# A half step by seven products: block columns first, a pinned order of products, norm parts from unshifted tokens

## The chip, the cores and the metric

One core of a Trainium2 chip runs the whole program in one launch. The metric is the device time of that launch in microseconds. TensorE multiplies; VectorE (DVE), ScalarE (ACT) and GpSimd (POOL) work on SBUF and, the first two, on PSUM; SyncE (SP) issues most DMAs, POOL some.

## The reference

Two layers over 256 context and 256 latent tokens of width 1024. Each layer is a SwiGLU half step, a token mixing (mLSTM and latent attention), and another half step; each part gets its tokens through a norm with shift and scale. What the change touches is one half step:

```python
def _rmsnorm(x, g):
    y = xf * lax.rsqrt(jnp.mean(xf * xf, axis=-1, keepdims=True) + EPS)
    return (y * g.astype(jnp.float32)).astype(x.dtype)

def _modulate(h, shift, scale):
    return h * (1 + scale) + shift

def _swiglu(h, w_up, w_dn):          # w_up 1024 x 5632, w_dn 2816 x 1024
    a, b = jnp.split(h @ w_up, 2, axis=-1)
    return (jax.nn.silu(a) * b) @ w_dn
...
x = x + 0.5 * mx[2] * _swiglu(_modulate(_rmsnorm(x, g_n1[l]), mx[0], mx[1]), w_ff1_up[l], w_ff1_dn[l])
ctx = ctx + 0.5 * mc[2] * _swiglu(_modulate(_rmsnorm(ctx, g_n1[l]), mc[0], mc[1]), w_ff1_up[l], w_ff1_dn[l])
```

## The kernel before

Tokens lie as columns: 512 of them, context 0 to 255 (CTX) and latent 256 to 511 (LAT), with the 1024 features as 8 blocks of 128 partitions. Every float32 operand is split into a high part and the rest (hh and hl for tokens, wh and wl for weights), and each product of two operands is three matmuls: high-high, high-low, low-high. A weight unit is loaded into a tile st (SP's queue, STB = 6 buffers, L49), then ScalarE copies it to wh and VectorE subtracts to get wl (L245 and L247, or L646 and L647 in parts7; WB = 4 buffers each, L48). Splits are given a higher priority than their place in the program (AHEAD, AHEAD_S), so that they run ahead of TensorE; the queue order on each engine is made by a list scheduler that goes by priority and by its own estimate of when inputs are there. Each engine then runs its queue in order.

The hidden width of 2816 is 22 block columns of 128. In the old form (up, L564) a block column is 2 halves (a and b) x 8 feature blocks x 3 matmuls, on all 512 tokens or, for the first two block columns of a half step, on the latent tokens first and then on the context, so that the latent ones can begin before the context's norm is done.

One half step, the first of the second layer (SEVEN, L44), does most block columns in another way (ff7, L772). It takes context and latent tokens as one 2 x 2 block matrix (stream by half of the features), the weights of two block columns as another (a11, a12, a21, a22), and computes the block product with seven multiplications in place of eight, by sums and differences of blocks. That is a Step (L679), two block columns at once. FIRST = 2 block columns go in the old form, STEPS = 10 steps follow, cut into CHUNKS of 2 + 2 x 3, 2 x 4 and 2 x 3 block columns; behind each chunk its part of the down product goes to all 8 output blocks (last_blocks, L513).

A product (L723) is 24 matmuls of 256 columns and adds to one of the step's three PSUM tiles: products 1, 6, 7 and 4 to the first, 2 and 3 to the second, 5 to the third. Its operands are: for 1, 2 and 3 the parts of the tokens themselves, for 5, 6, 7 and 4 differences of them (differences, L652; 4's overwrite the context part of hh). Its weights (L700): 1 is a11, 2 is a12, 5 is a21 + a22 (VectorE, L708), 6 is 5's tile with a11 added by a DMA with addition from POOL's queue (more, L696), 7 is 1's tile with a21 added, 3 is 6's tile with a12 added, 4 is a22. An addition must wait until the tile's earlier split is read. Behind 1, 6 and 7 ScalarE copies the first PSUM tile to SBUF (s, L753), and the next product into that tile waits for the copy. The written order of a step is 1, 2, (5 in the first step), 6, 5 of the next step, 7, 3, 4; the scheduler may run it in another.

The norm in front of this half step is shifted (L630): per feature block a scaled token block h (VectorE), the shift added in place (ScalarE), and after each second block the parts hh and hl from both at once, 512 columns (parts7). The other norms (norm_apply, L478) write hh straight from the scaled block with the shift as bias, and hl likewise, 256 columns at a time. In the last chunk last_blocks does its last `tail` output blocks stream by stream, latent first; the latent norm of the next part is issued behind the first context block.

Of the kernel before, what the change touches and what calls it, by code (L numbers as in the profile page):

```python
# [8 lines left out]
F32 = mybir.dt.float32  # L9
F32R = mybir.dt.float32r  # L10
I32 = mybir.dt.int32
AF = mybir.ActivationFunctionType
# [29 lines left out]
AHEAD = 150  # L42
AHEAD_S = 110
SEVEN = ((1, 0),)  # L44
FIRST = 2
STEPS = (FB - FIRST) // 2
CHUNKS = ((2, 3), (0, 4), (0, 3))
WB = 4  # L48
STB = 6  # L49
FEED = ((2, 10.5), (5, 10))  # L50
# [94 lines left out]
def body(ctx, tc, A):  # L145
# [15 lines left out]
    def psum(name="ps"):  # L161
        return pp.tile([P, 512], F32, tag="ps", name=name)
# [47 lines left out]
    def pair(n):  # L210

        if n <= HALF:
            t = act(F32R, "hl")
            return t[:, :n], t[:, HALF : HALF + n]
        return act(F32R, "hi")[:, :n], act(F32R, "lo")[:, :n]
# [35 lines left out]
    def units(keys, n, kb):  # L251

        res = []
        for key in keys:
            hi, lo = unit(key, n, kb)
            for k in range(kb):
                res.append((hi[:, k, :], lo[:, k, :]))
        return res
# [61 lines left out]
    def silu2(out, src):  # L320

        tanh_half(out, src)
        V.scalar_tensor_tensor(out, out, 1.0, src, ALU.add, ALU.mult)
# [114 lines left out]
    def mod(l, s, g, j):  # L438
        return mods[l, s][:, g * 8 + j : g * 8 + j + 1]
# [124 lines left out]
    def up(part, hp, up_keys, lhs, dst):  # L564

        w = part.stop - part.start
        pa, pb = psum("pa"), psum("pb")
        if lhs:
            mm3(pa[:, :w], lhs, hp, lsl=slice(0, P), late=True)
            flush()  # L570
            mm3(pb[:, :w], lhs, hp, lsl=slice(P, 2 * P), late=True)
        else:
            run(mmu([(pa[:, :w], slice(0, P), True), (pb[:, :w], slice(P, 2 * P), True)], up_keys, UW, 4, hp, turns=False))
        t = act(F32, "sg")[:, :w]
        silu2(t, pa[:, :w])
        V.scalar_tensor_tensor(t, t, 0.5, pb[:, :w], ALU.mult, ALU.mult)
        gh, gl = dst
        S.activation(gh, t, AF.Copy)
        V.tensor_tensor(gl, t, gh.bitcast(F32), ALU.subtract)
# [50 lines left out]
    def shifted(nm, l, s, g):  # L630

        r = nm.rstd()
        h = {}
        for a in range(2):
            for q in range(2):
                h[a, q] = t = act(F32, "h7")[:, :T].rearrange("p (k t) -> p k t", k=2)
                j0 = 4 * a + 2 * q
                for i in range(2):
                    j = j0 + i
                    V.scalar_tensor_tensor(t[:, i], xs[j][:, nm.cols], mod(l, s, g + 1, j), r, ALU.mult, ALU.mult)  # L640
                    S.activation(t[:, i], t[:, i], AF.Identity, bias=mod(l, s, g, j))
                parts7(t, hh[:, j0 : j0 + 2, nm.cols], hl[:, j0 : j0 + 2, nm.cols])
        hx[s] = h

    def parts7(t, hi, lo):
        S.activation(hi, t, AF.Copy)  # L646
        V.tensor_tensor(lo, t, hi.bitcast(F32), ALU.subtract)  # L647
# [31 lines left out]
    class Step:  # L679
# [40 lines left out]
            w = "p (b k n) -> p b k n"  # L720
            return hi.rearrange(w, b=2, k=4), lo.rearrange(w, b=2, k=4)

        def product(self, r):  # L723
            w = self.weights(r)
            b = {1: 1, 6: 1, 7: 1, 4: 1, 2: 2, 3: 2, 5: 3}[r]
            new = r in (1, 2, 5)
            if new:
                self.ps[b] = psum(f"r{b}")
            ps = self.ps[b]
            todo = [(k, p, x, y) for k in range(4) for p in range(2) for x, y in ((0, 0), (0, 1), (1, 0))]  # L730
            for i, (k, p, x, y) in enumerate(todo):
                TE.matmul(  # L732
                    ps[:, p * HALF : (p + 1) * HALF], w[x][:, p, k], hx["op", r][k][y],
                    start=new and i == 0, stop=i + 1 == len(todo), skip_group_check=True,
                )
            self.after(r)

        def tile(self, name):
            return act(F32, name)[:, :T]
# [8 lines left out]
        def after(self, r):  # L748
            v, ps = self.v, self.ps
            if r in (1, 6, 7):  # L750
                with tc.high_priority(offset=SOON):
                    v[r] = self.tile("s7")
                    S.activation(v[r], ps[1], AF.Copy)  # L753
                    if r == 6:
                        V.tensor_tensor(ps[2], ps[3], v[6], ALU.add)
            if r == 2:
                a, t = self.tile("a7"), self.tile("t7")
                with tc.high_priority(offset=SOON):
                    V.tensor_tensor(a, ps[2], v[1], ALU.add)
                silu2(t, a)  # L760
                v["lat"] = t
            elif r == 7:
                v["b"] = self.tile("b7")
                V.tensor_tensor(v["b"], ps[3], v[7], ALU.add)
            elif r == 3:
                v["ctx"] = self.tile("t7")
                silu2(v["ctx"], ps[2])
                self.out(0, v["ctx"], v["b"])
            elif r == 4:
                self.out(1, v["lat"], ps[1])  # L770

    def ff7(l, f, after):  # L772
        g0 = 0 if f == 0 else 6
        steps = [Step(l, f, t) for t in range(STEPS)]
        t0 = 0
        for c, (first, n) in enumerate(CHUNKS):
            gs = []
            if first:
                early = [(i, units([("up", l, f, i, u) for u in range(2)], UW, 4)) for i in range(first)]
                for s, part in ((1, LAT), (0, CTX)):  # L780
                    for i, lhs in early:
                        if s:
                            gs.append({})
                        hi, lo = pair(HALF)
                        up(part, hpairs(part), None, lhs, (hi, lo))
                        gs[i][s] = hi, lo
                        if s == 0:
                            if i == 0:
                                rest = differences()
                            next(rest, None)  # L790
            mine = steps[t0 : t0 + n]
            t0 += n
            for st in mine:
                st.product(1)
                st.product(2)
                if st.t == 0:
                    st.product(5)
                st.product(6)
                if st.t + 1 < STEPS:
                    steps[st.t + 1].product(5)  # L800
                st.product(7)
                st.product(3)
                st.product(4)
                gs += [{s: st.dst[s][i] for s in (0, 1)} for i in range(2)]

            def make(nb, c=c, nk=len(gs)):
                return units([("dn7", l, f, c, nb)], nk * P, nk)

            norms = {s: Norm((CTX, LAT)[s]) for s in (0, 1)} if c + 1 == len(CHUNKS) else None
            last_blocks(make, gs, [0, 1], l, g0 + 2, norms, lambda s: after(norms[s], s))  # L810


    def mix(l, after):
# [894 lines left out]
```

## Time and profile before

| | us |
|---|---|
| median of 3 runs | 2392.13 |
| range of the 3 runs | 2389.76 to 2392.64 |
| profiled execution | 2390.21 |
| its span, first to last instruction | 2388.5 |
| mean granted TensorE clock | 0.988 |

| engine | busy us | share of the span |
|---|---|---|
| TensorE matmul | 2318.5 | 97% |
| VectorE | 1675.8 | 70% |
| ScalarE | 1040.5 | 44% |
| GpSimd | 200.4 | 8% |

All times come from one profiled execution of the kernel. Busy time of TensorE is modelled, since matmuls overlap: one of 256 columns is shown with 0.28 us but the next starts after less than half of that. The granted clock is the share of the full TensorE clock (2.4 GHz) that was given in a stretch; 0.5 is 1.2 GHz. In a timeline the text in brackets is how long the engine was idle before the instruction and what released it.

### The profile page before, as it was taken

What the parts mean: (1) busy time and instruction counts of PE and PEld (TensorE: products, weight loads), DVE (VectorE), ACT (ScalarE), POOL (GpSimd) and SP (SyncE); (2) the same over time, 40 slices, a digit from 0 to 9 for tenths busy, and PEclk for the clock granted to TensorE, in tenths of its full rate; (3) what the DMA queues carried; (4) which work ended last, traced back from release to release, by engine and by line L of the source; (5) the groups of instructions that cost most, each with busy time, mean ns of one, the idle gap of its engine ahead of it and who ended that gap; (6) DMA issues with size and microseconds to landing.
All of it is one profiled execution on the core that took longest, in us unless ns stands there. A gap on an engine that the chain in (4) does not pass through costs nothing. (4 is left out here: it accounts for less than half of the span.)

```text
span 2388.5 us, 37179 instructions
## 1 busy us (share of the span) xinstructions
PE 2318.5 (97%) x14352; PEld 2053.4 (86%) x14352; DVE 1675.8 (70%) x3463; ACT 1040.5 (44%) x1698; POOL 200.4 (8%) x418
## 2 busy tenths in 40 slices
PE   8999999999999999999999997999999999999998
PEld 4888888888898888888888897999998898999998
DVE  6887777797577654479986666465667867776665
ACT  6322223567544442342222344253445664555443
POOL 1121110000010000021231001010100000000000
PEclk9999999999999999999999998999999999999999
DMA  9657445211222223465685436475633323355563
GB/s 336 199 161 230 156 144 162 81 64 55 70 80 71 80 73 95 133 203 178 216 291 175 128 86 138 127 172 134 151 97 92 96 82 106 105 167 160 168 209 103
DMA packets 104431, 332.83 MB, mean 139 GB/s; under 512 B 13502, under 2 KB 15806, under 8 KB 104254
## 3 DMA queue, kind: packets, MB, share of 16 engines
q1 hardware_dynamic: 79454, 247.61, 32.9%
q0 software_dynamic: 24800, 82.86, 12.5%
q8 instruction: 112, 1.84, 0.3%
q14 instruction: 65, 0.53, 0.1%
HBM read 327.27 MB, written 3.15 MB: 138 GB/s over the span
## 5 line engine op out<-in xcount | busy, mean ns | idle before, releaser
L245 ACT ACTIVATE wh<-st 128x1024 fp32r<-128x1024 f32 (+3 forms) x436 | 427.5, 983 | 801.3 <-issue 237.3
L247 DVE TENSOR_TENSOR wl<-st,wh 128x1024 fp32r<-128x1024 f32 (+3 forms) x436 | 490.3, 1127 | 269.4 <-ACT wh L245 267.1
L385 POOL DMA_DIRECT2D ada<-ada x256 | 137.3, 538 | 740.1 <-PE dn L267 215.9
L292 PE MATMUL p<-hl,wh 128*128 128x256 f32 (+1 forms) x536 | 179.4, 335 | 0.0
L267 PE MATMUL dn<-hi,wl 128*128 128x512 f32 (+1 forms) x476 | 174.3, 366 | 0.0
L267 PE MATMUL dn<-hi,wh 128*128 128x512 f32 (+1 forms) x476 | 173.9, 367 | 0.0
L291 PE MATMUL p<-hh,wh 128*128 128x512 f32 (+1 forms) x512 | 173.5, 339 | 0.0
L267 PE MATMUL dn<-lo,wh 128*128 128x512 f32 (+1 forms) x476 | 173.4, 365 | 0.0
L293 PE MATMUL p<-hh,wl 128*128 128x512 f32 (+1 forms) x512 | 172.5, 337 | 0.0
L293 PE MATMUL pb<-hh,wl 128*128 128x512 f32 (+1 forms) x480 | 171.0, 356 | 0.0
L291 PE MATMUL pa<-hh,wh 128*128 128x512 f32 (+1 forms) x480 | 171.0, 356 | 0.0
L292 PE MATMUL pa<-hl,wh 128*128 128x512 f32 (+1 forms) x480 | 171.0, 356 | 0.0
L291 PE MATMUL pb<-hh,wh 128*128 128x512 f32 (+1 forms) x480 | 171.0, 356 | 0.0
L292 PE MATMUL pb<-hl,wh 128*128 128x512 f32 (+1 forms) x480 | 171.0, 356 | 0.0
L293 PE MATMUL pa<-hh,wl 128*128 128x512 f32 (+1 forms) x480 | 171.0, 356 | 0.0
L396 DVE SCALAR_TENSOR_TENSOR ada<-ada,cs 128x512 f32<-128x512 f32 x256 | 166.6, 683 | 0.0
L502 DVE SCALAR_TENSOR_TENSOR x<-dn,mod,x 128x256 f32<-128x256 f32 x152 | 68.2, 478 | 101.5 <-PE dn L267 51.4
L646 ACT ACTIVATE wh<-st 128x1024 fp32r<-128x1024 f32 x70 | 73.8, 1059 | 127.9 <-issue 43.1
L396 DVE SCALAR_TENSOR_TENSOR junk<-ada,cs 128x512 f32<-128x512 f32 x192 | 123.5, 683 | 0.0
L647 DVE TENSOR_TENSOR wl<-st,wh 128x1024 fp32r<-128x1024 f32 x70 | 85.2, 1221 | 47.8 <-ACT wh L646 47.8
L292 PEld LDWEIGHTS p<-hl,wh 128*128 128x128 f32 x536 | 100.7, 188 | 11.0
L293 PEld LDWEIGHTS p<-hh,wl 128*128 128x128 f32 x512 | 96.1, 188 | 11.3
(418 smaller groups left out, 6305.8 us busy)
## 6 DMA issues: line engine op xcount, KB each, us to landing
st<-wall SPq DMA_DIRECT2D x356, 512.0 KB, 3.6
ada<-ada POOLq DMA_DIRECT2D x256, 256.0 KB, 3.7
st<-wall SPq DMA_DIRECT2D x64, 384.0 KB, 3.1
st<-wall SPq DMA_DIRECT2D x48, 320.0 KB, 2.9
st<-wall POOLq DMA_DIRECT2D x30, 512.0 KB, 5.5
ada<-ada SPq DMA_DIRECT2D x32, 256.0 KB, 5.5
x<-xT SPq DMA_DIRECT2D x8, 256.0 KB, 5.5
cb<-cc SPq DMA_DIRECT2D x8, 256.0 KB, 6.0
```

What stands on the lines that cost most here:

```text
L245: S.activation(hi[:, :n], st[:, :n], AF.Copy)
L247: V.tensor_tensor(lo[:, :n], st[:, :n], hi[:, :n].bitcast(F32), ALU.subtract)
L267: TE.matmul(ps, lhs[k][a][:, lsl], rhs[k][b][:, rsl], start=i == 0, stop=i == 3 * n - 1)
L291: TE.matmul(ps, a, b, start=first, stop=False)
L292: TE.matmul(ps, a, bl, start=False, stop=False)
L293: TE.matmul(ps, al, b, start=False, stop=final_)
L385: nc.gpsimd.dma_start(st, ada[ADA[l, g] + j, :, q * 512 : (q + 1) * 512])
L396: V.scalar_tensor_tensor(o, st, 0.5, cb[s, q], ALU.mult, ALU.mult, accum_out=dst)
L502: V.scalar_tensor_tensor(xs[nb][:, cols], ps[:, pcols], mod(l, s, g, nb), xs[nb][:, cols], ALU.mult, ALU.add)
L646: S.activation(hi, t, AF.Copy)
L647: V.tensor_tensor(lo, t, hi.bitcast(F32), ALU.subtract)
```

## The change

Four block columns go in the old form instead of two, the first two as before, the other two on all 512 tokens; nine steps follow. The chunks become 4 + 2 x 1, 2 x 4 and 2 x 4 block columns. The first differences are made behind the second early block column, those for product 4 behind the fourth. The first matmul of every product is put behind the last of the product before it, so the written order holds: 5, 1, 2, 6, next 5, 7, 3, 4 in the first step; 1, 2, 6, next 5, 7, 3, 4 in the others; in the last but one, the last step's 1 goes ahead of 4; the last is 6, 2, 7, 3, 4. The sum that prepares the second PSUM tile (L755) is done behind the later of 2 and 6. In the norm, hh is written from the unshifted block with the shift as bias, hl likewise, block by block; the shift is added in place behind all blocks. The stream-by-stream tail of last_blocks has three output blocks there instead of two.

```diff
-FIRST = 2
+FIRST = 4
 STEPS = (FB - FIRST) // 2
-CHUNKS = ((2, 3), (0, 4), (0, 3))
+CHUNKS = ((4, 1), (0, 4), (0, 4))
...
                     V.scalar_tensor_tensor(t[:, i], xs[j][:, nm.cols], mod(l, s, g + 1, j), r, ALU.mult, ALU.mult)
-                    S.activation(t[:, i], t[:, i], AF.Identity, bias=mod(l, s, g, j))
-                parts7(t, hh[:, j0 : j0 + 2, nm.cols], hl[:, j0 : j0 + 2, nm.cols])
+                    hi, sh = hh[:, j, nm.cols], mod(l, s, g, j)
+                    S.activation(hi, t[:, i], AF.Identity, bias=sh)
+                    V.scalar_tensor_tensor(hl[:, j, nm.cols], t[:, i], sh, hi.bitcast(F32), ALU.add, ALU.subtract)
+        for (a, q), t in h.items():
+            for i in range(2):
+                S.activation(t[:, i], t[:, i], AF.Identity, bias=mod(l, s, g, 4 * a + 2 * q + i))
...
-        def product(self, r):
+        def product(self, r, mark):
...
             for i, (k, p, x, y) in enumerate(todo):
-                TE.matmul(
+                with tc.issue_after(mark) if mark and i == 0 else nullcontext():
+                    mm = TE.matmul(
...
             self.after(r)
+            return mm.ins
...
-                    if r == 6:
-                        V.tensor_tensor(ps[2], ps[3], v[6], ALU.add)
             if r == 2:
-                a, t = self.tile("a7"), self.tile("t7")
+                v[2] = self.tile("a7")
                 with tc.high_priority(offset=SOON):
-                    V.tensor_tensor(a, ps[2], v[1], ALU.add)
-                silu2(t, a)
-                v["lat"] = t
+                    V.tensor_tensor(v[2], ps[2], v[1], ALU.add)
+            if r in (2, 6) and 2 in v and 6 in v:
+                with tc.high_priority(offset=SOON):
+                    V.tensor_tensor(ps[2], ps[3], v[6], ALU.add)
+            if r == 2:
+                v["lat"] = self.tile("t7")
+                silu2(v["lat"], v[2])
...
-                early = [(i, units([("up", l, f, i, u) for u in range(2)], UW, 4)) for i in range(first)]
+                keys = [[("up", l, f, i, u) for u in range(2)] for i in range(first)]
+                early = [(i, units(keys[i], UW, 4)) for i in range(2)]
...
-                        if s == 0:
-                            if i == 0:
-                                rest = differences()
-                            next(rest, None)
+                        if s == 0 and i == 1:
+                            rest = differences()
+                            next(rest)
+                for i in range(2, first):
+                    gs.append(pair(T))
+                    up(slice(0, T), hpairs(slice(0, T)), keys[i], None, gs[i])
+                next(rest, None)
+                gs[2:] = [{s: [x[:, (CTX, LAT)[s]] for x in g] for s in (0, 1)} for g in gs[2:]]
...
-                st.product(1)
-                st.product(2)
-                if st.t == 0:
-                    st.product(5)
-                st.product(6)
-                if st.t + 1 < STEPS:
-                    steps[st.t + 1].product(5)
-                st.product(7)
-                st.product(3)
-                st.product(4)
+                t = st.t
+                order = [(t, 1), (t, 2), (t, 6), (t + 1, 5), (t, 7), (t, 3), (t, 4)]
+                if t == 0:
+                    order.insert(0, (t, 5))
+                if t == STEPS - 2:
+                    order.insert(6, (t + 1, 1))
+                if t == STEPS - 1:
+                    order = [(t, 6), (t, 2), (t, 7), (t, 3), (t, 4)]
+                for u, r in order:
+                    mark = steps[u].product(r, mark)
...
-            last_blocks(make, gs, [0, 1], l, g0 + 2, norms, lambda s: after(norms[s], s))
+            last_blocks(make, gs, [0, 1], l, g0 + 2, norms, lambda s: after(norms[s], s), 3)
```

## Rows read from the trace of the kernel before

**Rows 1.** the page: share of TensorE, and its granted clock in 40 slices, in tenths.

```profile
PE 2318.5 (97%) x14352; PEld 2053.4 (86%) x14352; DVE 1675.8 (70%) x3463; ACT 1040.5 (44%) x1698; POOL 200.4 (8%) x418
PEclk9999999999999999999999998999999999999999
```

**Rows 2.** windows: us, busy us (x count) of PE, PEld, DVE, ACT, POOL, clock, DMA, GB/s.

```profile
1395.40:1425.00 29.60, 26.53 (x198) 25.86 (x197) 22.27 (x42) 18.76 (x39) 0.06 (x1) 0.88 0.16 51
1425.00:1459.90 34.90, 22.54 (x150) 21.36 (x149) 22.56 (x31) 13.15 (x19) 4.27 (x5) 0.76 0.55 122
1459.90:1771.50 311.60, 305.27 (x2574) 303.21 (x2573) 187.76 (x238) 129.00 (x169) 22.56 (x27) 1.00 0.59 146
1771.50:1784.00 12.50, 8.60 (x48) 8.11 (x46) 10.92 (x24) 6.92 (x14) 0.00 (x0) 0.73 0.17 48
```

**Rows 3.** TensorE's waits from 1380 to 1780: waiter, releaser, us, times, longest.

```profile
PE r L732 <- ACT s L753: 11.7, 8, 6.2
PE r L732 <- ACT wh L646: 5.5, 2, 4.6
PE cq L267 <- ACT hh L485: 3.9, 1, 3.9
```

**Rows 4.** chain of waits, a product; timeline of TensorE, first and last of eleven.

```profile
1734.96 2.80 PE r L732 x24
...
1047.79 0.39 PE L291 MATMUL pa<-hh,wh 128*128 128x512 f32 x1
1050.12 0.40 PE L292 MATMUL pa<-hl,wh 128*128 128x512 f32 x1
```

**Rows 5.** timeline, start of the half step; windows of two like starts.

```profile
1395.11 0.49 ACT L641 ACTIVATE h<-h,mod 128x256 f32<-128x256 f32 x1
1397.37 0.61 ACT L646 ACTIVATE hh<-h 128x512 fp32r<-128x512 f32 x1
...
1398.04 0.48 PE L267 MATMUL pa<-hh,wh 128*128 128x256 f32 x1 [2.46 <-ACT hh L646]
...
414.00:420.00 6.00, 5.08 (x39) 4.72 (x39) 6.00 (x13) 4.39 (x11) 0.00 (x0) 1.00 0.59 207
1021.00:1031.10 10.10, 7.94 (x54) 7.10 (x54) 9.95 (x24) 5.77 (x13) 5.84 (x11) 1.00 0.79 263
```

**Rows 6.** groups by form, VectorE, 1390 to 1780: count, busy us, mean ns.

```profile
L640 DVE SCALAR_TENSOR_TENSOR h<-x,mod,rstd 128x256 f32<-128x256 f32 x16 | 6.6, 478 | 0.1
L647 DVE TENSOR_TENSOR hl<-h,hh 128x512 fp32r<-128x512 f32 x8 | 5.2, 684 | 0.2 <-ACT hh L646 0.2
```

**Rows 7.** timeline of POOL, ScalarE and TensorE in the first step.

```profile
1428.75 0.86 POOL L697 DMA_DIRECT2D st<-wall  x1 [2.90 <-DVE wl L647]
...
1436.22 2.95 ACT L646 ACTIVATE wh<-st 128x1024 fp32r<-128x1024 f32 x3 [3.91 <-DMA st<-wall]
1444.32 1.06 ACT L646 ACTIVATE wh<-st 128x1024 fp32r<-128x1024 f32 x1 [4.63 <-DMA st<-wall]
1449.39 0.58 ACT L753 ACTIVATE s<-r 128x512 f32<-128x512 f32 x1
...
1438.28 0.58 PE L732 MATMUL r<-dh,wh 128*128 128x256 f32 x1 [4.58 <-ACT wh L646]
1450.03 0.58 PE L732 MATMUL r<-dh,wh 128*128 128x256 f32 x1 [6.19 <-ACT s L753]
```

**Rows 8.** windows of two triples of products and of the last step.

```profile
1557.50:1566.20 8.70, 8.70 (x74) 8.57 (x73) 5.48 (x6) 4.19 (x5) 0.17 (x1) 1.00 0.68 194
1577.40:1586.80 9.40, 8.77 (x74) 8.57 (x73) 5.75 (x7) 4.08 (x5) 0.17 (x1) 1.00 0.71 192
1725.00:1741.00 16.00, 13.55 (x112) 12.96 (x111) 8.93 (x11) 7.11 (x10) 0.00 (x0) 1.00 0.40 120
```

**Rows 9.** a window and the longest wait of TensorE in the mixing that follows.

```profile
1840.00:1890.00 50.00, 45.28 (x313) 41.38 (x312) 47.42 (x102) 30.34 (x57) 2.25 (x4) 0.97 0.32 96
...
1878.79 0.66 PE L1419 MATMUL pT<-consts,pr 128*128 128x128 f32 x4 [4.49 <-ACT pr L1405]
```

More of the change, by code (lines that the diff above doesn't have):

```diff
@@ L727, in product @@
             if new:
-                self.ps[b] = psum(f"r{b}")
+                self.ps[b] = psum("r" + "ABC"[b - 1])
             ps = self.ps[b]
@@ L731, in product @@
             for i, (k, p, x, y) in enumerate(todo):
-                TE.matmul(
-                    ps[:, p * HALF : (p + 1) * HALF], w[x][:, p, k], hx["op", r][k][y],
-                    start=new and i == 0, stop=i + 1 == len(todo), skip_group_check=True,
-                )
+                with tc.issue_after(mark) if mark and i == 0 else nullcontext():
+                    mm = TE.matmul(
+                        ps[:, p * HALF : (p + 1) * HALF], w[x][:, p, k], hx["op", r][k][y],
+                        start=new and i == 0, stop=i + 1 == len(todo), skip_group_check=True,
+                    )
             self.after(r)
+            return mm.ins
         def tile(self, name):
@@ L751, in after @@
                 with tc.high_priority(offset=SOON):
-                    v[r] = self.tile("s7")
+                    v[r] = self.tile("s" + "abc"[(1, 6, 7).index(r)])
                     S.activation(v[r], ps[1], AF.Copy)
-                    if r == 6:
-                        V.tensor_tensor(ps[2], ps[3], v[6], ALU.add)
             if r == 2:
-                a, t = self.tile("a7"), self.tile("t7")
+                v[2] = self.tile("a7")
                 with tc.high_priority(offset=SOON):
-                    V.tensor_tensor(a, ps[2], v[1], ALU.add)
-                silu2(t, a)
-                v["lat"] = t
+                    V.tensor_tensor(v[2], ps[2], v[1], ALU.add)
[5 more added lines that the diff above has]
+                silu2(v["lat"], v[2])
             elif r == 7:
@@ L774, in ff7 @@
         steps = [Step(l, f, t) for t in range(STEPS)]
-        t0 = 0
+        t0, mark = 0, None
         for c, (first, n) in enumerate(CHUNKS):
```

## The prediction

> **What bounds the kernel now.** I read the page first: TensorE is busy 97% of the span at a granted clock of 9 tenths nearly throughout [rows 1], so time can only come from fewer columns of matmul, from TensorE's idle stretches, or from stretches at the lower clock. The half step that is changed lies between 1395.4 us and about 1784 us. So I cut just that stretch into four windows [rows 2]: the old-form block columns (1395.4 to 1425.0), the first step's products (to 1459.9), the other steps and the down products (to 1771.5), and the end with the start of the mixing (to 1784). A product is 24 matmuls and takes 2.80 us, 0.1167 us each [rows 4]; windows count their matmuls, so length minus count times 0.1167 is what each window loses:
>
> - first window, 198 matmuls: 29.6 - 23.1 = **6.5 us**, clock 0.88
> - second, 150: 34.9 - 17.5 = **17.4 us**, clock 0.76
> - third, 2574: 311.6 - 300.4 = **11.2 us**, clock 1.00
> - fourth, 48: 12.5 - 5.6 = **6.9 us**, clock 0.73
>
> The waits say who causes it [rows 3]: 11.7 us for the evacuation s (L753), 5.5 us for a split weight wh (L646), 3.9 us at the end for hh of the mixing's norm. The rest of the loss is half clock after idle stretches: the three windows with long waits are those whose mean clock is below 1. VectorE is busy 188 of 312 us in the third window, ScalarE 129 [rows 2], so neither bounds the steps.
>
> **The change part by part.**
>
> *One step fewer, two block columns more.* A step goes: 7 products x 24 = 168 matmuls of 256 columns, 168 x 0.1167 = 19.6 us. Two block columns come: 2 x 48 matmuls of 512 columns; ten of these start over 2.33 us [rows 4], 0.233 each, so 22.4 us. TensorE's work grows by **2.8 us**. The down products have 22 blocks in all either way, only cut 6, 8, 8 for 8, 8, 6. No row can hide this: it is the bound engine.
>
> *Norm parts.* Now a bias in place (ScalarE, 256 columns) precedes a copy of 512 columns that makes hh; the first hh therefore comes from the second of two bias instructions and the copy at 1397.37, and TensorE starts at 1398.04 after 2.46 us of idleness [rows 5]. After the change the first instruction, at 1395.11 for 0.49 us, writes hh itself: 1395.6, about when the last down product ends. The price is VectorE's: hl in 16 pieces of 256 columns, taken like the 478 ns of the L640 form, instead of 8 of 684 ns [rows 6]: 16 x 0.478 - 8 x 0.684 = 2.2 us over both streams, beside TensorE; ScalarE gets 16 deferred biases of about 0.49 for 8 copies of 0.61, 3.0 us more, also beside TensorE. The same form of norm already starts two other stages: 414 to 420 loses 6.0 - 39 x 0.1167 = 1.4 us, 1021 to 1031.1 loses 10.1 - 54 x 0.1167 = 3.8 us, both at clock 1.00 [rows 5]. So the bounds for what stays of 6.5 us are 1.4 and 6.5 (no gain, if the deferred biases delay the context's parts and the clock falls anyway); I take the mean of the two like stages, 2.6: **-3.9 us** (-5.1 to 0).
>
> The Trainium skill (VectorE: DVE Perf Modes, section The TRN2 errata) speaks against this part: memory latency shows between instructions, so tiles of 512 elements or more are advised. The trace agrees with the direction, since 478 ns for half of what takes 684 ns is dearer per element [rows 6]; by that rule alone this part costs its 2.2 us instead of giving 3.9, and the sum would be 6 us higher.
>
> *The first step behind four block columns.* Now the first step begins as soon as the two early block columns end. Its order is 1, 2, 5, 6; product 6 needs the tile of product 5 with another quarter added by a DMA from POOL's queue. That was issued at 1428.75, ScalarE could split its result only at 1436.22, up to 7.5 us later, and TensorE stood 4.58 us [rows 7]. Next, ScalarE stood 4.63 us in front of another such DMA (1444.32) with the evacuation s behind it in its queue, which came at 1449.39; TensorE stood 6.19 us [rows 7]. After the change the 96 wide matmuls, 22.4 us, lie between, and weights come four units ahead (WB = 4): the split of product 5 can go when the first of the four new weight units is used up, some 5.6 us into these 22.4, and its DMA (7.5 us) has landed 9 us before product 5 starts; product 6 comes three products later. The addition for 7 waits for the split of 1 and has likewise over 10 us. The differences for 5, 6, 7 are made during the wide matmuls too, the one for 4 after them, eight products ahead of use. The four new units queue on SP before the step's loads, POOL carries only the additions. Left over: between 0 and one wait like the 4.58; I take 1.5: **-15.9 us** (-17.4 to -12.8). If this cover were gone the whole 17.4 would stay.
>
> *Products in the written order.* Pinning adds no semaphore, only order on TensorE; if a product stands, all later products and the down products placed behind it stand as well. Now the scheduler runs, in most steps, the next step's 5 before 6, then 7 directly behind 6. Both use one PSUM tile, and 7 stands until s of 6 is out: 1577.4 to 1586.8, 74 matmuls, loses 9.4 - 8.6 = 0.76 us; there are six such triples. In two steps just behind a down phase the order was 6, 5, 7, and 1557.5 to 1566.2, also 74 matmuls, loses 0.06 [rows 8]. The written order is this one in all of the eight steps that have a next 5. I take 0.25 each, since s can still stand behind a weight split in ScalarE's queue: 6 x 0.76 + 2 x 0.06 - 8 x 0.25 = **-2.7 us** (8 x 0.06 gives -4.2, 8 x 0.76 gives +1.4). Each addition gets more room: 3 now follows 6 by three products instead of two. In the last step, 1 goes ahead of the previous 4, and 2 stands between 6 and 7: of 16.0 - 112 x 0.1167 = 2.9 us lost from 1725 to 1741 [rows 8] I leave 0.9: **-2.0 us** (-2.9 to 0).
>
> *The end.* The last chunk has 8 blocks and the last three outputs go stream by stream. The latent norm's sums now come after the first context block; behind them were 18 matmuls, 2.1 us, before TensorE ran dry for 3.9 us [rows 3]; afterwards 48, 5.6 us. At 414 the same chain had 33 matmuls, 3.9 us, behind it, and lost 1.4 us without a drop of the clock [rows 5]. I leave 1.4 of 6.9: **-5.5 us** (-6.9 to -3.0). Three weight units instead of two are held to the end, so one of four is free for the mixing's first weights; the second unit's turn comes 5.6 us before the end, enough for its 1.06 us split [rows 7] and the subtraction.
>
> *What comes back.* The mixing starts with VectorE less far ahead; from 1840 to 1890 VectorE is busy 47.4 of 50 us, and TensorE stands 4.49 us there [rows 9]. I take **+2.0 us** (0 to +4.5).
>
> Sum: 2.8 - 3.9 - 15.9 - 2.7 - 2.0 - 5.5 + 2.0 = -25.2 us. The profiled execution took 2390.21 us (its span 2388.5 us), 0.08% below the median of 2392.13; 2390.2 - 25.2 = 2365.0, forecast **2365**. With all bounds good 2356.5, all bad 2383; since they don't hang together I give the forecast alone 2357 to 2376.
>
> **The rivals.**
> 1. *The end gives nothing.* VectorE is busy 10.9 of the last window's 12.5 us [rows 2] and full later in the mixing [rows 9]. If it sets the mixing's pace from the start, the 5.5 us come back as longer waits: 2365.0 + 5.5 = about **2370**. Against it: those 10.9 us hold the norms of both streams, which are over once, and TensorE stood in their middle, so they were not all needed first. Chance 0.12.
> 2. *The gap of 6 and 7 stays.* Both keep one PSUM tile and ScalarE's queue decides: 8 x 0.76 instead of 2.0, **2369**. Chance 0.10. The Trainium skill (Perfetto Trace Analysis, Optimization Strategy) reads a gap that repeats alike on the busy engine as a possible lack of buffers; by that rule order wouldn't cure it. The trace disagrees for the two triples with 5 between, which have the same tiles.
> 3. *The change doesn't do what it says in the first step*, because the scheduler places the loads or splits late in SP's or ScalarE's queue: the 15.9 stay lost, **2381**. Chance 0.07.
> 4. *Slower:* with the order pinned, nothing can run in front of a late addition. If every step stood as product 6 did, 9 x 4.58 = 41 us, **2406**; it passes the old time from 3.0 us a step. For it: 7.5 us of landing is nearly three products. Against it: in the third window additions ran as closely, and of 5.5 us for wh all but 0.9 is the one wait of the first step [rows 3]. Chance 0.07, of which 0.03 for a price that ends near the old time.
>
> **How the numbers follow.** The forecast has 0.64. Its own range, rivals 1 and 2 lie inside 2356 to 2377; out of it are rivals 3 and 4 and a rest of the forecast, under 0.2 in all. A measurement of this kernel tells about 0.2% from no change; forecast and rivals 1 to 3 are all faster by more: 0.93; rival 4 gives 0.03 same, 0.04 slower.
>
> **What would show it.** Right: no wait over 2 us of a product for wh or s, clock 1.00 from the wide block columns to the end, triples without 0.6 us waits, TensorE's idle before the first cq under 1.5 us, 1512 (9 x 168) product matmuls. Wrong: ScalarE waiting for an st DMA with s behind it in several steps, TensorE standing before the wide matmuls, or longer waits in the mixing than the 4.49 us.

## The result and the profile after

The changed kernel takes 2361.3 us (median of 4 runs, 2359.66 to 2362.74) against 2391.03 us of the kernel before in the same series: ratio 0.9875, 95% interval 0.9858 to 0.9892, 29.7 us less. The forecast was 2365. The profiled execution took 2362.57 us, its span is 2360.8 us.

Share of TensorE and its granted clock, from the page of the changed kernel, against [rows 1]:

```profile
PE 2309.6 (98%) x14280; PEld 2043.9 (87%) x14280; DVE 1673.3 (71%) x3464; ACT 1039.7 (44%) x1700; POOL 198.2 (8%) x415
PEclk9999999999999999999999999999999999999999
```

No slice is below 9 tenths any more. Then the same four stretches as [rows 2], at the places where they now lie (windows; columns as there): old-form block columns, of these the wide ones by themselves in the second row, all products and down products, the end with the start of the mixing.

```profile
1398.10:1425.30 27.20, 26.15 (x198) 25.10 (x198) 23.34 (x50) 20.85 (x47) 0.00 (x0) 0.94 0.26 78
1425.30:1447.70 22.40, 22.40 (x98) 18.00 (x98) 17.25 (x24) 10.29 (x16) 1.76 (x2) 1.00 0.52 132
1447.70:1744.30 296.60, 296.60 (x2522) 296.60 (x2521) 186.17 (x235) 127.89 (x165) 22.60 (x27) 1.00 0.60 148
1744.30:1762.00 17.70, 16.78 (x131) 16.03 (x131) 16.40 (x34) 11.10 (x20) 0.00 (x0) 1.00 0.30 89
```

With 0.1167 us a matmul (0.233 for the 96 wide ones) the losses are: first 27.2 - 23.1 = 4.1 us (before 6.5); second 22.4 - 22.4 = 0, and the first step's 17.4 us have no successor; third 296.6 - 2522 x 0.1167 = 2.3 us (before 11.2); fourth 17.7 - 131 x 0.1167 = 2.4 us (before 6.9). The clock is 1.00 from the wide block columns on. TensorE's waits from 1380 to 1900 us, columns as [rows 3]:

```profile
PE pT L1433 <- ACT pr L1419: 6.8, 1, 6.8
PE kn L267 <- ACT hi L924: 1.6, 1, 1.6
PE rope L1110 <- ACT qz L1369: 1.2, 1, 1.2
PE pa L267 <- ACT hh L642: 1.0, 1, 1.0
PE cq L267 <- DVE hl L486: 0.9, 1, 0.9
```

No product is in the list. What is left of the half step is a gap of 1.0 us at its start and one of 0.9 us at its end; the rest belongs to the mixing, where the longest wait has grown from 4.49 us [rows 9] to 6.8.

To compare kernels I use one length from the timeline of TensorE: from the start of the last down matmul in front of the half step to the first kn matmul that waits 1.55 us in the mixing. It leaves out what an execution gains or loses elsewhere. Before:

```profile
1395.30 0.28 PE L267 MATMUL dn<-lo,wh 128*128 128x256 f32 x1
...
1826.33 0.51 PE L267 MATMUL kn<-hi,wh 128*128 128x512 f32 x1 [1.55 <-ACT hi L910]
```

After, with the long wait of the mixing as well:

```profile
1397.93 0.28 PE L267 MATMUL dn<-lo,wh 128*128 128x256 f32 x1
...
1797.64 0.50 PE L267 MATMUL kn<-hi,wh 128*128 128x512 f32 x1 [1.55 <-ACT hi L924]
...
1852.35 1.11 PE L1433 MATMUL pT<-consts,pr 128*128 128x128 f32 x4 [6.80 <-ACT pr L1419]
```

That is 431.03 us before and 399.71 after, **31.3 us less**. The half step began 2.6 us later in the profiled execution of after, and the stretch from kn to pT is 54.71 us instead of 52.46; that leaves 26.4 of the 31.3 us, and the span fell by 27.7, the last 1.3 us coming from elsewhere.

### The profile page after: what moved, and what is told of

The parts are those of the page before. It is cut to its first block, busy times and chain, and to the rows that moved or that the text cites. A ratio compares the mean times of both kernels' runs of the same rounds, so it can differ in the third digit from the quotient of the medians.

```text
span 2360.8 us, 37038 instructions
## 1 busy us (share of the span) xinstructions
PE 2309.6 (98%) x14280; PEld 2043.9 (87%) x14280; DVE 1673.3 (71%) x3464; ACT 1039.7 (44%) x1700; POOL 198.2 (8%) x415
## 4 chain that ended last, share of the span: by engine, by line
PE 93%; DVE 3%; ACT 2%; issue 1%; DMA 1%; DVEq 0%; SPq 0%; ACTq 0%
PE dn L267 16%; PE dn L508 5%; PE rA L738 4%; PE pb L293 4%; PE pa L293 4%; PE pb L292 4%; PE pa L292 4%; PE pb L291 4%; PE pa L291 4%; PE p L291 4%; PE p L292 4%; PE p L293 4%; PE rB L738 2%; PE pv L267 2%; PE pa L267 2%; PE pb L267 2%
## 5 line engine op out<-in xcount | busy, mean ns | idle before, releaser
L247 DVE TENSOR_TENSOR wl<-st,wh 128x1024 fp32r<-128x1024 f32 (+3 forms) x440 | 495.4, 1128 | 268.0 <-ACT wh L245 265.3
L293 PE MATMUL pb<-hh,wl 128*128 128x512 f32 (+1 forms) x496 | 177.4, 358 | 0.0
L291 PE MATMUL pb<-hh,wh 128*128 128x512 f32 (+1 forms) x496 | 177.4, 358 | 0.0
L292 PE MATMUL pb<-hl,wh 128*128 128x512 f32 (+1 forms) x496 | 177.4, 358 | 0.0
L292 PE MATMUL pa<-hl,wh 128*128 128x512 f32 (+1 forms) x496 | 177.4, 358 | 0.0
L293 PE MATMUL pa<-hh,wl 128*128 128x512 f32 (+1 forms) x496 | 177.4, 358 | 0.0
L291 PE MATMUL pa<-hh,wh 128*128 128x512 f32 (+1 forms) x496 | 177.4, 358 | 0.0
L650 ACT ACTIVATE wh<-st 128x1024 fp32r<-128x1024 f32 x63 | 66.9, 1061 | 97.5 <-PE dn L508 31.4
L292 PEld LDWEIGHTS pb<-hl,wh 128*128 128x128 f32 x496 | 93.0, 188 | 15.5
L293 PEld LDWEIGHTS pb<-hh,wl 128*128 128x128 f32 x496 | 93.0, 188 | 15.4
```

What stands on the lines that cost most here:

```text
L247: V.tensor_tensor(lo[:, :n], st[:, :n], hi[:, :n].bitcast(F32), ALU.subtract)
L291: TE.matmul(ps, a, b, start=first, stop=False)
L292: TE.matmul(ps, a, bl, start=False, stop=False)
L293: TE.matmul(ps, al, b, start=False, stop=final_)
```

## The experiments

Each was timed beside the kernel before on one chip, in five series; the median of the kernel before lay between 2390.7 and 2391.8 us in them, so a difference between two medians of different series is good to no better than about 1 us. "Stage" is the length just defined, from the one profiled execution of each kernel; slow_chain, whose edit lies in the mixing, repeats the changed kernel's within 0.4 us. "kn to pT" is the stretch behind it. Line numbers in the rows (L738 and so on) are those of the kernel that the row is from.

| kernel | median us | ratio to before, interval | stage us | kn to pT us |
|---|---|---|---|---|
| changed | 2361.3 | 0.9875 (0.9858 to 0.9892) | 399.7 | 54.7 |
| undo_blocks | 2368.6 | 0.9902 (0.9887 to 0.9917) | 407.0 | 52.5 |
| undo_pin | 2370.4 | 0.9910 (0.9895 to 0.9925) | 406.1 | 54.4 |
| undo_tail | 2365.0 | 0.9887 (0.9871 to 0.9904) | 402.1 | 52.5 |
| undo_norm | 2363.5 | 0.9886 (0.9871 to 0.9900) | 402.3 | 54.4 |
| blocks_alone | 2377.6 | 0.9943 (0.9930 to 0.9957) | 412.0 | 52.5 |
| order_alone | 2376.1 | 0.9939 (0.9927 to 0.9951) | 414.5 | 52.5 |
| no_add_step0 | 2387.0 | 0.9979 (0.9970 to 0.9988) | 424.9 | 54.3 |
| no_diff | 2379.9 | 0.9955 (0.9943 to 0.9968) | 417.4 | 54.5 |
| long_first | 2367.7 | 0.9897 (0.9884 to 0.9911) | 402.3 | 54.4 |
| slow_chain | 2363.9 | 0.9886 (0.9871 to 0.9901) | 400.1 | - |
| gated | 2361.1 | 0.9876 (0.9863 to 0.9890) | 397.5 | 54.4 |
| five_later | 2377.6 | 0.9947 (0.9933 to 0.9961) | 413.0 | 54.3 |

### One part undone

**undo_blocks**

```diff
-FIRST = 4
+FIRST = 2
...
-CHUNKS = ((4, 1), (0, 4), (0, 4))
+CHUNKS = ((2, 2), (0, 4), (0, 4))
```

> The changed kernel (2361.3 us) with two block columns in the old form again, ten steps, chunks of 2 + 2 x 2, 2 x 4, 2 x 4; pinned order, norm parts and tail as changed. Theory (the cover of the wide block columns is what ended the first step's loss): TensorE has 2.8 us less to do, but splits that are queued behind late additions let products of the first step stand again, 8 to 17 us at half clock; 2361 - 2.8 + 13 = about 2371, between 2366 and 2376. Rival (the pinned order with 5 first, which puts three products between 5 and 6, ended that loss): only the 2.8 us are left, 2358.5.

Measured: 7.3 us slower than the changed kernel, 7.25 us in the stage, although TensorE has 2.8 us less to do; so the wide block columns cover 10 us. That is inside the theory's range and far from the rival's 2358.5. But the waits are others than I had named:

```profile
PE rC L738 <- ACT dh L650: 4.2, 1, 4.2
PE rA L738 <- ACT sa L760: 2.1, 1, 2.1
```

The first product, now 5, waits for the parts of a difference (dh), and a later one for the evacuation of product 1 (sa). No wait of TensorE names a split. But an addition has a share in the first one: in ScalarE's queue the dh that 5 waits for, at 1426.68, stands behind a split for which ScalarE stood 1.62 us, until 6's addition had landed:

```profile
1425.42 1.06 ACT L650 ACTIVATE wh<-st 128x1024 fp32r<-128x1024 f32 x1 [1.62 <-DMA st<-wall]
```

**undo_pin**

```diff
-                    mark = steps[u].product(r, mark)
+                    steps[u].product(r, None)
```

> The changed kernel (2361.3 us) without the pin; the program still writes 6 ahead of the next 5. Theory (the pin is what keeps 5 between 6 and 7): in the steps parts of 5 are placed ahead of 6 again, 7 follows 6 closely and waits for s about 0.7 us in eight steps, 2361.3 + 6 = 2367. Rival (the order written in the program is enough, or s is never late once the first step is covered): 2361.3, within 2 us.

Measured: 9.1 us slower, 6.35 us of it in the stage. The scheduler put the first 10 or 11 matmuls of the next 5 ahead of 6 in three steps, the other 13 or 14 between 6 and 7; in the five other steps it put 16 ahead of 6 and only 8 between, and four of these five have the wait for sb, the evacuation of 6. Waits from 1440 to 1745 us, and one such place in the timeline:

```profile
PE rA L738 <- ACT sb L760: 2.5, 4, 0.6
PE rA L738 <- ACT sa L760: 1.2, 1, 1.2
PE dn L508 <- ACT wh L245: 1.0, 1, 1.0
...
1534.66 0.39 PE L738 MATMUL rA<-dh,wh 128*128 128x256 f32 x1 [0.62 <-ACT sb L760]
1534.90 0.28 PE L738 MATMUL rA<-dl,wh 128*128 128x256 f32 x1
```

At each of the four sb waits the product's first matmul starts late and its second again 0.24 us later instead of 0.117, so one place costs about 0.9 us. In the kernel before it is the same: at the triple of [rows 8] the last matmul of 6 starts at 1582.98, the first of 7 at 1583.88 and its second at 1584.11.

```profile
1583.88 0.39 PE L732 MATMUL r<-dh,wh 128*128 128x256 f32 x1 [0.63 <-ACT s L753]
```

The 0.76 that I had read there was too low because the window counts 74 matmuls and a triple has 72; the other two began ahead of it. The order written in the program isn't enough, the pin is needed; the theory holds, and its 6 us are what the stage shows, a third less than the median. But the four waits make only 3.6 of them; the waits for sa (1.2 us) and for a down matmul's split (1.0) come back as well. Of the median's 9.1 us, 2.7 lie outside the stage, and I don't know where.

**undo_tail**

```diff
-            last_blocks(make, gs, [0, 1], l, g0 + 2, norms, lambda s: after(norms[s], s), 3)
+            last_blocks(make, gs, [0, 1], l, g0 + 2, norms, lambda s: after(norms[s], s))
```

> The changed kernel (2361.3 us) with two instead of three output blocks done stream by stream at the end. Theory (cover behind the latent norm's sums sets the end): 24 matmuls, 2.8 us, instead of 48, 5.6 us, lie behind the first context block; TensorE stands about 3 us more before the mixing and runs some us at half clock, 2361.3 + 5 = 2366. Rival (what is saved there is given back in the mixing, where VectorE is full): 2361.3, within 2 us, with the longest wait of the mixing back to 4.5 us from 6.8.

Measured: 3.7 us slower, 2.4 in the stage. The intervals of the two ratios overlap, so the waits decide:

```profile
PE pT L1433 <- ACT pr L1419: 4.5, 1, 4.5
PE cq L267 <- ACT hh L485: 2.2, 1, 2.2
```

The wait in front of cq is 2.2 us instead of 0.9, as the theory has it; the mixing's long wait is back to 4.5 us, as the rival has it. Both are true at once, but the one doesn't follow from the other: undo_blocks has the short wait in front of cq and the short one of the mixing, and no_add_step0, below, has 3.9 us in front of cq and 6.5 in the mixing. In undo_blocks:

```profile
PE pT L1433 <- ACT pr L1419: 4.6, 1, 4.6
PE cq L267 <- DVE hl L486: 0.9, 1, 0.9
```

**undo_norm**

```diff
-                    hi, sh = hh[:, j, nm.cols], mod(l, s, g, j)
-                    S.activation(hi, t[:, i], AF.Identity, bias=sh)
-                    V.scalar_tensor_tensor(hl[:, j, nm.cols], t[:, i], sh, hi.bitcast(F32), ALU.add, ALU.subtract)
-        for (a, q), t in h.items():
-            for i in range(2):
-                S.activation(t[:, i], t[:, i], AF.Identity, bias=mod(l, s, g, 4 * a + 2 * q + i))
+                    S.activation(t[:, i], t[:, i], AF.Identity, bias=mod(l, s, g, j))
+                parts7(t, hh[:, j0 : j0 + 2, nm.cols], hl[:, j0 : j0 + 2, nm.cols])
```

> The changed kernel (2361.3 us) with the old norm parts: bias in place and copies of 512 columns. Theory (the parts from unshifted tokens bring the first matmul forward): the first matmul of the half step waits 2.4 us instead of under 1, and the stretch at half clock grows from about 3 to 7 us, 2361.3 + 2.5 = 2364. Rival by VectorE's time (256-column instructions cost 2.2 us more): 2359 to 2360.

Measured: 2.2 us slower, 2.6 in the stage; the theory's 2364. The intervals of the two ratios overlap, so the stage decides: the first matmul waits 2.5 us again.

```profile
PE pa L267 <- ACT hh L646: 2.5, 1, 2.5
```

### One part alone

**blocks_alone** is the kernel before with the four block columns, the wide loop and the new chunks; products, norm and tail are the old ones.

```diff
-FIRST = 2
+FIRST = 4
-CHUNKS = ((2, 3), (0, 4), (0, 3))
+CHUNKS = ((4, 1), (0, 4), (0, 4))
...
+                for i in range(2, first):
+                    gs.append(pair(T))
+                    up(slice(0, T), hpairs(slice(0, T)), keys[i], None, gs[i])
```

> The kernel before (2391 us) with the four block columns and the chunks 4 + 2 x 1, 2 x 4, 2 x 4 alone; products unpinned in the old written order, norm parts and tail as before. Theory (the wide block columns cover the first step by themselves): the second stretch's 17.4 us of loss fall under 3, TensorE does 2.8 us more, 2391 - 14.5 + 2.8 = 2379, between 2376 and 2382. Rival (cover helps only with the pinned order): the first step still shows a wait over 4 us and the time is above 2385.

**order_alone** is the kernel before with the new product and after functions and the new order, pinned. The first differences, too, are made where the changed kernel makes them, behind the second early block column and not behind the first.

```diff
-            for st in mine:
-                st.product(1)
...
+                order = [(t, 1), (t, 2), (t, 6), (t + 1, 5), (t, 7), (t, 3), (t, 4)]
...
+                for u, r in order:
+                    mark = steps[u].product(r, mark)
```

> The kernel before (2391 us) with the pinned order alone; two block columns, ten steps, old chunks, norm parts and tail. Theory (order takes the gaps out of the steps, some 6 us, and about a third of the first step's 17.4 us, since the additions are three products further off there): 2391 - 12 = 2379, with a wait of about 4 us for the differences left. Rival (the order only takes out the gaps of 0.7 us): 2385 or more.

Measured: 2377.6 and 2376.1 us, both within 3 us of what was expected. Alone they bring 14.1 us (blocks) and 15.7 us (order and pin); undone from the changed kernel, the blocks are worth 7.3 us and the pin by itself 9.1. They overlap, since each ends a part of the same first step's loss; so the four parts undone one by one add up to 22.3 us and not to 29.7. With the blocks alone the first 34 us of the products lose 33.9 - 272 x 0.1167 = 2.2 us, and one wait over 1 us is left in them, but the gaps of the steps are all there:

```profile
1448.10:1482.00 33.90, 32.07 (x272) 31.83 (x272) 22.21 (x30) 15.74 (x23) 1.71 (x2) 1.00 0.51 125
...
PE r L732 <- ACT s L753: 6.3, 7, 1.8
```

With the order alone the gaps are gone, and product 5, which comes first, waits for its difference, longer than the 4 us that I had expected:

```profile
PE rC L734 <- ACT dh L646: 6.8, 1, 6.8
```

### What the first step's loss is made of

undo_blocks and order_alone, where TensorE waits for differences, speak against my reading of [rows 7], in which late additions stop the first step. So I took away first the additions and then the differences, each from the kernel before.

**no_add_step0**

```diff
-            nc.gpsimd.dma_start(self.st[n], self.src(q), accum_op=ALU.add)
+            if self.t:
+                nc.gpsimd.dma_start(self.st[n], self.src(q), accum_op=ALU.add)
```

> The kernel before (2391 us) without the three added DMAs of step 0 (products 6, 7 and 3 of that step multiply the tile as it stands, so that part of the product isn't the reference's). Theory (in the first step ScalarE's queue stands in front of late additions): the waits of 4.6 and 6.2 us go, the clock stays up, 2391 - 12 = 2379. Rival (the buffers of split weights come free late and the differences are late, whatever the additions do): the waits stay, 2391, within 3 us.

**no_diff**

```diff
-        d = {}
-        makes = (
...
+        for r in (5, 6, 7):
+            hx["op", r] = hx["op", 1]
+        yield
+        hx["op", 4] = hx["op", 3]
```

> The kernel before (2391 us) without the differences of the tokens: products 5, 6, 7 take the operand of 1, product 4 that of 3, so the half step's result isn't the reference's; matmuls, loads and additions are unchanged. After the run without the additions of the first step, 13 of its 17.4 us of loss are still open. Theory (the eight difference tiles and their parts fill VectorE's and ScalarE's queues, and the evacuation of product 1 stands behind them): the waits of 4.6 and 6.2 us shrink to under 3 in all, 2391 - 10 = 2381. Rival (it is the order of ScalarE's queue and the splits of the first weights alone): 2388 or more, with a wait for s over 4 us.

The same window of 35 us, 1425 to 1460, has room for 300 matmuls at 0.1167 us. Its row in the kernel before, in no_add_step0 and in no_diff (columns as [rows 2]):

```profile
1425.00:1460.00 35.00, 22.64 (x151) 21.46 (x150) 22.56 (x31) 13.15 (x19) 4.27 (x5) 0.76 0.56 122
```

```profile
1425.00:1460.00 35.00, 25.49 (x196) 24.89 (x195) 25.26 (x34) 16.57 (x24) 1.76 (x2) 0.85 0.38 96
```

```profile
1425.00:1460.00 35.00, 32.71 (x267) 32.28 (x266) 22.53 (x26) 17.27 (x24) 6.05 (x7) 0.95 0.71 162
```

The losses are 35.0 - 151 x 0.1167 = 17.4 us, 12.1 us without additions, 3.8 us without differences. The median falls by 4.8 and by 11.5 us. So the theory of the additions falls for the greater part (its rival, which had the time within 3 us of 2391, doesn't hold either), and that of the differences holds. The two amounts, 5.3 and 13.6 us, add up to more than 17.4, so what they cost overlaps. Without additions a wait of 8.5 us for s takes the place of two:

```profile
PE r L733 <- ACT s L754: 8.5, 1, 8.5
PE r L733 <- ACT wh L646: 1.0, 1, 1.0
```

Without differences the evacuation s of product 1 runs at 1430.26, as soon as its product ends, and then ScalarE stands 5.49 us in front of an addition, with TensorE waiting for 1.9 us of it at most:

```profile
PE r L716 <- ACT wh L646: 2.3, 2, 1.9
...
1430.26 0.60 ACT L737 ACTIVATE s<-r 128x512 f32<-128x512 f32 x1 [0.26 <-PE r L716]
1436.34 2.95 ACT L646 ACTIVATE wh<-st 128x1024 fp32r<-128x1024 f32 x3 [5.49 <-DMA st<-wall]
```

So the additions are late, but only with the differences in the program do s and the next splits lie far behind in ScalarE's queue. no_diff takes away both the time of the differences and their places in the queue, and doesn't tell which counts: a run with the differences in it and s ahead of them wasn't made. ScalarE's instructions of the kernel before, in the order in which they were compiled, show the same place (the list of the program, not the trace; SW1, SW0 and SW2 are additions, HW a load):

```
L646 wh<-st     waits for DMA SW1, PE      (split that waits for an addition)
L646 wh<-st     waits for PE, ACT          (next step's 5: its 4.58 us wait)
L646 wh<-st     waits for DMA SW0, PE, ACT
L646 dh<-d      waits for DVE              (part of a difference)
L646 wh<-st     waits for DMA SW2, PE, ACT
L646 dh<-d      waits for DVE
L318 sg<-pa
L646 wh<-st     waits for DMA HW5, PE, ACT
L578 hl<-sg     waits for DVE
L753 s<-r                                  (evacuation of product 1, 6.19 us wait)
```

The product that stood 4.58 us was the next step's 5, whose own tile needs no addition; its split stood behind one that does. The product that stood 6.19 us was 6, waiting for the evacuation of 1.

**five_later** asks whether another order of the first step could do without the wide block columns.

```diff
 # on undo_blocks
-                    order.insert(0, (t, 5))
+                    order.insert(2, (t, 5))
```

> The kernel of undo_blocks (2368.6 us: two block columns, ten steps, all else as changed) with product 5 of the first step behind 1 and 2 instead of ahead of them. Theory (without the wide block columns the differences are late, and 5, which needs them, stood 4.2 us when it came first): 1 and 2 give 5.6 us of cover, the wait of 5 goes, but 6 now comes right behind 5 and stands for its addition, 2 to 5 us; 2363 to 2369. Rival (the first step needs no wide block columns, only another order, so the 2.8 us of TensorE work are saved): 2358 to 2360, faster than the changed kernel.

Measured: 2377.6 us, 9 us slower than undo_blocks and well above both forecasts. The window from 1425 to 1460 of order_alone, undo_blocks and five_later:

```profile
1425.00:1460.00 35.00, 27.48 (x208) 26.98 (x207) 27.71 (x39) 17.84 (x25) 4.77 (x6) 0.85 0.67 151
```

```profile
1425.00:1460.00 35.00, 29.77 (x221) 29.28 (x222) 27.06 (x36) 18.56 (x26) 3.87 (x5) 0.85 0.59 137
```

```profile
1425.00:1460.00 35.00, 22.34 (x155) 21.55 (x154) 22.97 (x33) 14.46 (x20) 3.43 (x4) 0.76 0.51 112
```

They lose 10.7, 9.2 and 16.9 us. In five_later 5 waits for its difference all the same, after half of its matmuls, and 6 waits longer than in the kernel before:

```profile
PE rA L738 <- ACT sa L760: 6.9, 1, 6.9
PE rC L738 <- ACT dh L650: 4.6, 1, 4.6
```

5.6 us of matmuls ahead of 5 didn't help, since on ScalarE the second half of its difference then stood behind three splits, of which the first waited 3.73 us for 6's addition:

```profile
1431.36 2.95 ACT L650 ACTIVATE wh<-st 128x1024 fp32r<-128x1024 f32 x3 [3.73 <-DMA st<-wall]
1434.21 0.61 ACT L650 ACTIVATE dh<-d 128x512 fp32r<-128x512 f32 x1
```

So an addition does hold up the first step here, by way of the queue, as one held up 5's difference for 1.62 us in undo_blocks. No order that I tried does without the cover. But order_alone, undo_blocks and five_later all make the first differences one block column later than the kernel before; the new order with the old place of the differences wasn't tried.

### The end of the half step and the mixing

**long_first**

```diff
-CHUNKS = ((4, 1), (0, 4), (0, 4))
+CHUNKS = ((4, 2), (0, 4), (0, 3))
```

> The changed kernel (2361.3 us) with chunks 4 + 2 x 2, 2 x 4, 2 x 3, so the short chunk is last. Theory (behind the latent norm's sums 36 matmuls, 4.2 us, instead of 48, 5.6 us, are just about enough): 2361.3 + 1 = 2362, at most 2364. Rival (a short last chunk costs what a tail of two costs): 2365.

Measured: 6.4 us slower, where I had expected at most 3. The wait in front of cq is 2.5 us, like that of the tail of two:

```profile
PE pT L1433 <- ACT pr L1419: 6.4, 1, 6.4
PE cq L267 <- ACT hh L485: 2.5, 1, 2.5
```

So the short last chunk costs what a tail of two costs, and the rival is right, at least in the stage (+2.6 us, undo_tail +2.4). The other 3.8 us of the median lie outside the stage; they stay open.

**slow_chain**

```diff
-SLOW = (3, 2)
+SLOW = (3, 1)
```

> The changed kernel (2361.3 us) with the gate chain of the second layer's mixing drawn at every pump instead of at every second (SLOW = (3, 1)). Theory (the longest wait of the mixing, 6.8 us for pr, is set by when the gate chain's VectorE instructions are queued): it shrinks by some 3 us, 2358. Rival (VectorE is full there, so its work only changes places): 2361, within 2 us, with the wait moved elsewhere.

Measured: 2363.9 us, 2.6 us above the changed kernel, not 3 below. The wait of 6.8 us is gone and others stand in its place, of which this is the longest; from kn to the end of the span it takes 3.3 us more than the changed kernel.

```profile
PE sc L1410 <- DVE hl L1128: 4.0, 1, 4.0
```

The longer wait of the mixing isn't caused by what the half step does with its end. In thirteen of the fourteen programs that stretch has just two lengths, 52.5 us (kernel before, undo_blocks, undo_tail, blocks_alone, order_alone) and 54.3 to 54.7 us (all others but slow_chain, where the pT wait doesn't exist). VectorE's first 260 groups of instructions of the mixing, as compiled, are those of the kernel before, or nearly, in the first group of programs (0 lines of difference, some 30 in order_alone), and nearly those of the changed kernel in the second (10 lines at most, over 100 from the kernel before). no_add_step0 and no_diff have the old end and the second order. So the 2.25 us go with the order in which the scheduler queues VectorE's work, not with a VectorE that comes less far ahead. That the order causes them is argued from this agreement; no run changes the order alone.

### The start of the half step

**gated** puts the splits of the second early block column behind the latent stream's parts.

```diff
+                    mark2 = S.activation(hi, t[:, i], AF.Identity, bias=sh)
...
+        marks7.append((mark2.ins, mark.ins))
...
+                gates.extend([(None, None), (None, None), marks7[0], marks7[0]])
                 early = [(i, units(keys[i], UW, 4)) for i in range(2)]
```

> The changed kernel (2361.3 us) with the splits of the second early block column's weights put behind the last hh of the latent stream on ScalarE and behind the last scaled block on VectorE. Theory (a weight split of 1.06 us between the first and the second hh makes the first gap, after which the clock falls for some 3 us): the 0.97 us gap goes and the clock stays at 1.00, 2361.3 - 2.5 = 2359. Rival (the second block column's weights then come late and TensorE stands later): 2361 to 2363.

In the changed kernel a weight split runs between the first and the second hh, and TensorE, having used the first, waits:

```profile
1397.74 0.49 ACT L642 ACTIVATE hh<-h,mod 128x256 fp32r<-128x256 f32 x1
1398.24 1.06 ACT L245 ACTIVATE wh<-st 128x1024 fp32r<-128x1024 f32 x1
1399.21 2.89 ACT L642 ACTIVATE hh<-h,mod 128x256 fp32r<-128x256 f32 x7
...
1399.75 0.39 PE L267 MATMUL pa<-hh,wh 128*128 128x256 f32 x1 [0.97 <-ACT hh L642]
```

The two windows of 4 us from there on, first of the changed kernel, then of gated:

```profile
1398.00:1402.00 4.00, 2.95 (x15) 2.03 (x14) 4.00 (x10) 3.99 (x9) 0.00 (x0) 0.95 0.55 186
1402.00:1406.00 4.00, 4.00 (x21) 3.82 (x22) 4.00 (x9) 2.22 (x6) 0.00 (x0) 0.62 0.43 123
```

```profile
1398.00:1402.00 4.00, 3.86 (x24) 3.22 (x25) 4.00 (x12) 4.00 (x9) 0.00 (x0) 1.00 0.05 20
1402.00:1406.00 4.00, 4.00 (x35) 3.94 (x34) 3.40 (x5) 3.97 (x11) 0.00 (x0) 1.00 0.21 27
```

The gap goes, the clock stays at 1.00, 59 matmuls run in 8 us instead of 36 (55 at the same distance from the last down matmul, since gated began 1.2 us earlier), and the stage is 2.2 us shorter (397.5 us). The median, 2361.1 us, isn't: from pT to the end gated takes 2.3 us more than the changed kernel. The mechanism at the start is shown; a faster kernel isn't.

## Why the prediction was right, point by point

The sign, the range and the main parts were right; 2365 was 3.7 us too high, and two causes were wrong: what had stopped the first step, and what comes back in the mixing.

- **Work of TensorE, +2.8 us.** Right: the 96 wide matmuls take 22.4 us, the 9 x 168 products run at 0.1167.
- **Norm parts, -3.9 us.** The first window gives 6.5 - 4.1 = 2.4 us, undo_norm 2.2 (2.6 in the stage). The step that failed is the likeness to the starts in [rows 5]: those kept the full clock, this one fell to a mean of 0.62 from 1402 to 1406, after the gap of 0.97 us that the split between the first two hh makes. By the advice against smaller tiles (the Trainium skill, VectorE: DVE Perf Modes, The TRN2 errata) this part would have lost 2.2 us; undo_norm, which takes the smaller tiles and the earlier first hh back together and is 2.2 us slower, disagrees.
- **First step, -15.9 us.** All 17.4 went. The size was right because the wide block columns cover whatever is late (blocks_alone leaves 2.2 us); the cause that I gave was right only for the smaller part: I read the additions into [rows 7]. Without them 12.1 us of the loss stay, without the differences 3.8. I also took the product that stood 4.58 us for 6; it was the next 5, queued behind an addition's split. The line "the differences are made during the wide matmuls too" was the important one, and I gave it no price.
- **Written order, -2.7 and -2.0 us.** The third window's loss fell from 11.2 to 2.3, 8.9 us; undo_pin says 6.35 in the stage and 9.1 in the median. The terms that were mis-sized: I left 0.25 us to each triple, and none is left; and a triple without the pin costs 0.9 us, not 0.76, since the window of [rows 8] counts two matmuls too many. Rival 2, the gap that stays because of the shared PSUM tile, is refuted. So is, for this gap, the reading of a repeating gap as a possible lack of buffers (the Trainium skill, Perfetto Trace Analysis, Optimization Strategy): undo_pin has the same buffers, and the order alone brings the gap back.
- **The end, -5.5 us.** 6.9 - 2.4 = 4.5 us by the windows; undo_tail gives 3.7 (2.4 in the stage, the last chunk having 8 blocks there). The chunk order is part of this term: long_first shows that it matters as much as the tail.
- **What comes back, +2.0 us.** 2.25 us came back, but not by the cause that I gave: they go with the order of VectorE's queue, not with its lead, so the size was right by luck. A wait of the mixing longer than 4.49 us was one of my signs of being wrong, and it came (6.8 us). Rival 1 is wrong in its mechanism.
- **Rivals 3 and 4.** No product waits, so neither did the first step's loss stay nor did late additions stop every step: the third window, with nearly all of the additions in it, loses 2.3 of 296.6 us.

By windows the sum is 2.8 - 2.4 - 17.4 - 8.9 - 4.5 = -30.4 us, near the 31.3 us of the stage; my terms for the same parts added up to -27.2. The order gave 4.2 us more than forecast and the first step 1.5, the norm parts 1.5 and the end 1.0 less.

## What to carry to other kernels

When a wait names a split or an evacuation, take away each thing queued ahead of it, one at a time, before believing the one that looks slow: here the DMA with addition looked guilty, and taking it away gave back under a third of the loss. Matmul groups that need nothing new are good cover where a stage changes its operands; here 22.4 us of them, at a price of 2.8, ended 10 us of loss behind the new order (undo_blocks) and 15 us by themselves (blocks_alone). A product order that a scheduler may change isn't an order; pin it where two products share a PSUM tile.

## What the runs showed of the hardware

A short gap can be followed by the lower clock where a longer one isn't: in the changed kernel TensorE's gap of 0.97 us and a stretch of 15 matmuls in 4 us were followed by a mean clock of 0.62 (full 2.4 GHz is 1.00, the lower level 0.5), while 1021 to 1031.1 us stayed at 1.00 [rows 5] behind a gap of 2.16 us. TensorE's wait there, from the timeline of the kernel before:

```profile
1023.17 0.39 PE L267 MATMUL pa<-hh,wh 128*128 128x256 f32 x1 [2.16 <-ACT hh L485]
```

The shorter gap was the one that the half clock followed; what else has to come with it, the runs don't show. A matmul that starts after a wait in the steps is followed by the next one after 0.23 to 0.24 us (1583.88 in the kernel before, 1534.66 in undo_pin), not 0.117.
